# Two-block transformer on one core: products with weights' rounded parts first, and weight splits held behind a norm's scalings

## The chip, the cores and the metric

The kernel runs on one core of a Trainium2 chip. The time is the device time of one execution in microseconds (us). The engines that matter are TensorE (PE in the profile, its weight loads PEld), VectorE (DVE), ScalarE (ACT), GpSimd (POOL) and SyncE (SP), which issues the weight loads from memory.

## The reference, cut to what matters

A batch of one with 256 positions of width 1024 goes through two layers of a first block (retention and a sparse attention with three branches, then a gated feed-forward of 2816) and two layers of a second block (three attentions A, B and C, then a feed-forward of 4096 and a gated embedding). All is float32. What sets the time is the chain of projections, each of the form `norm(x) @ W` or `f @ W`:

```python
h = rms_norm(x, norm_mix_g[i])
proj = h @ w_in[i]
...
x = x + mixed.astype(x.dtype)
h = rms_norm(x, norm_ffn_g[i])
a, b = jnp.split(h @ w_ffn_in[i], 2, axis=-1)
x = x + ((jax.nn.silu(a) * b) @ w_ffn_out[i]).astype(x.dtype)
```

## The kernel before, in words

**Products.** Every float32 weight and activation is split into a rounded high part and a low part, the rest. ScalarE copies the high part out (`whi` of a weight), and VectorE subtracts it to get the low part (`wlo`): lines 172 and 186, function `split`. A product `x @ W` is then three TensorE products in the faster float32 mode: x high by w high, x low by w high (both need `whi` alone), and x high by w low (needs `wlo`). All TensorE products stand at line 219, transposes at line 253. "High products" are below those with `whi`, "low products" those with `wlo`.

**Items.** The kernel is first written down as a list of items, each one weight tile of 128x1024 numbers (512 KB) and the products that use it: `proj_T`, `proj_T2`, `proj_N`, `proj_H` and `Down` make them. `execute` walks over the list. Ahead of item i it loads and splits weights of later items: up to LOOK = 2 beyond the current one, with five buffers for loaded weights (NB_RAW), freed by the low part, and six for split ones (NB_HI), and at a norm's turn at most PAST_TURN = 3 past it. `proj_T2` makes the two feed-forwards' first products: per tile of 128x128 a high product of 512 columns (x high and x low side by side in `HL`) and a low product of 256 columns.

**Norms.** `Down.ends` finishes a projection back into x. Its second column half comes for rows t=0 first (four items with weights) and then for rows t=1 (four items that reuse them). After each, `norm().add(t, 1, ...)` adds to x on VectorE, squares on ScalarE, lets GpSimd raise to the power -1/2 (line 242) and scales x on VectorE (`scale`, line 197, two instructions that make `w`). `turn(t)` then transposes the scaled rows on TensorE and splits them into x high (ScalarE) and x low (VectorE), both in `xt`. `turn(0)` stands before the last item of t=1; `turn(1)` before the last of the four t=0 items of the next projection. That next projection is written with rows t=0 first and t=1 after (`tmajor`), and its t=1 half begins five products after the transposes of `turn(1)`.

**Order.** Attention heads and the like are generators ("beside") that are pumped after each item, by a planner that adds up costs per engine (`eng`). The framework lays each engine's instructions out in one fixed queue, by the order written and by its own estimate of what is ready; `tc.issue_after(q)` puts what it encloses behind q on q's engine. Each engine then takes its queue in that order.

Of the kernel before, what the change touches and what calls it, by code (L numbers as in the profile page):

```python
# [82 lines left out]

LOOK, PAST_TURN = 2, 3
CMP_STEP, RAW_LOOK = 3, 6
TAIL = 8
BEHIND = 3
# [13 lines left out]
def tile_kernel(ctx: ExitStack, tc: tile.TileContext, A: dict, out: bass.AP):  # L103
# [254 lines left out]
    def do(fn, *a):  # L358
        items.append(Item(lambda pc: fn(*a)))

    order_after = []
    raw_free = [0.0] * NB_RAW

    def arrival():
# [29 lines left out]
    def execute():  # L394
        n = len(items)
        raws = [i for i in range(n) if items[i].spec is not None and items[i].spec[-1]]
        specs = [i for i in range(n) if items[i].spec is not None and not items[i].spec[-1]]
        end = {i: i for i in specs}
        for i, it in enumerate(items):
            if it.held is not None:  # L400
                end[it.held] = i
        nxt, live = 0, []
        for i, it in enumerate(items):
            live = [j for j in live if end[j] >= i]
            while raws and raws[0] <= i + RAW_LOOK:
                j = raws.pop(0)
                items[j].pc = load(items[j].spec)
            while nxt < len(specs) and i >= lead:
                j = specs[nxt]
                ahead = sum(1 for q in specs[max(0, nxt - LOOK - 8):nxt] if q >= i)  # L410
                if items[j].pc is None:
                    items[j].pc = load(items[j].spec)
                if j > i and (len(live) >= NB_HI or ahead > LOOK):
                    break
                turn = next((q for q in turns if i <= q < j), None)
                if turn is not None and sum(1 for q in specs if turn < q < j) >= (FIRST if turn == lead else PAST_TURN):
                    break
                items[j].pc = split_weight(items[j].pc, items[j].spec)
                live.append(j)
                nxt += 1  # L420
            it.fn(it.pc)
            if it.spec is not None or it.held is not None:
                bg.pump()
# [37 lines left out]
    def proj_T2(w2d, c0, x, evac):  # L461


        box = {}
        for k0 in range(0, 8, 4):
            def fn(pc, k0=k0):
                if k0 == 0:
                    box["b"] = [bank([128, 2, 256]) for _ in range(2)]
                hi, lo = pc
                for k in range(4):  # L470
                    kk = k0 + k
                    for ct in range(2):
                        cs = slice(128 * ct, 128 * ct + 128)
                        o = box["b"][ct]
                        mm(o, hi[:, k, cs], S[x].HL(kk), kk == 0, False)
                        mm(o[:, 0, :], lo[:, k, cs], S[x].H(kk), False, kk == 7)
                if k0:
                    evac(box["b"])

            items.append(Item(fn, spec(w2d, 128 * k0, 4, c0, 256)))  # L480
# [8 lines left out]
    def proj_T(w2d, c0, ncols, x, nkt, evac, r0=0, runs=1, stride=0, pre=None):  # L489


        cw = 256 // runs
        for ci, c in enumerate(range(0, ncols, cw)):
            box = {}
            for k0 in range(0, nkt, 4):
                nk = min(4, nkt - k0)

                def fn(pc, ci=ci, k0=k0, nk=nk, box=box):
                    if pre is not None:
                        pre(k0)  # L500
                    if k0 == 0:
                        box["b"] = bank([128, 2, 256])
                    hi, lo = pc
                    xx = S[x]
                    for k in range(nk):
                        kk = k0 + k
                        for ct in range(2):
                            cs = slice(128 * ct, 128 * ct + 128)
                            wh, wl = hi[:, k, cs], lo[:, k, cs]
                            o = box["b"][:, ct, :]  # L510
                            mm(o, wh, xx.H(kk), kk == 0 and ct == 0, False)
                            mm(o, wh, xx.L(kk), False, False)
                            mm(o, wl, xx.H(kk), False, kk == nkt - 1)
                    if k0 + nk == nkt:
                        evac(ci, box["b"])

                items.append(Item(fn, spec(w2d, r0 + 128 * k0, nk, c0 + c, cw, runs, stride)))

    def part_N(acc, xx, kk, nkt, t, pc, k, first):
        hi, lo = pc  # L520
        s = slice(128 * t, 128 * t + 128)
        mm(acc, xx.H(kk)[:, s], hi[:, k, :], first, False)
        mm(acc, xx.H(kk)[:, s], lo[:, k, :], False, False)
        mm(acc, xx.L(kk)[:, s], hi[:, k, :], False, kk == nkt - 1)

    def proj_N(w2d, c0, c, x, nkt, evac, runs=1, stride=0, tmajor=False, between=None, turn=None, pre=None):

        n = c * runs
        npk = 1024 // n
        box = {}
        ks = [(k0, min(npk, nkt - k0)) for k0 in range(0, nkt, npk)]
        held = []

        def fn(pc, j, k0, nk, tt_):
            if tmajor and j == len(ks) - 1 and tt_ == (0,) and between is not None:
                between()
            if pre is not None:  # L540
                pre(k0)
            for t in tt_:
                if k0 == 0:
                    box[t] = bank([128, n])
                for k in range(nk):
                    part_N(box[t], S[x], k0 + k, nkt, t, pc, k, k0 + k == 0)
                if k0 + nk == nkt:
                    evac(t, box[t])

        for j, (k0, nk) in enumerate(ks):  # L550
            items.append(Item(lambda pc, a=(j, k0, nk): fn(pc, *a, (0,) if tmajor else (0, 1)),
                              spec(w2d, 128 * k0, nk, c0, c, runs, stride)))
            held.append(len(items) - 1)
        if tmajor:
            for j, (k0, nk) in enumerate(ks):
                if j == len(ks) - 1 and turn is not None:
                    turn()
                items.append(Item(lambda pc, a=(j, k0, nk), src=items[held[j]]: fn(src.pc, *a, (1,)), None, held[j]))

    def proj_H(w2d, c0, ncols, x, nkt, evac):  # L560

        for ci, c in enumerate(range(0, ncols, 256)):
            box = {}
            for k0 in range(0, nkt, 4):
                def fn(pc, ci=ci, k0=k0, box=box):
                    if k0 == 0:
                        box["b"] = bank([128, 2, 256])
                    for t in range(2):
                        for k in range(4):
                            part_N(box["b"][:, t, :], S[x], k0 + k, nkt, t, pc, k, k0 + k == 0 and t == 0)  # L570
                    if k0 + 4 == nkt:
                        evac(ci, box["b"])

                items.append(Item(fn, spec(w2d, 128 * k0, 4, c0 + c, 256)))

    class Down:

# [3 lines left out]
            self.w, self.n, self.tail = w2d, nkt, tail  # L581
            self.acc = None

        def part(self, k, f, pc, kk, t, c, cs):
            if self.acc is None:
                self.acc = [[bank([128, 512]) for _ in range(2)] for _ in range(2)]
            hi, lo = pc
            s = slice(128 * t, 128 * t + 128)
            o = self.acc[t][c]
            mm(o, f.H(k)[:, s], hi[:, kk, cs], k == 0, False)  # L590
            mm(o, f.H(k)[:, s], lo[:, kk, cs], False, False)
            mm(o, f.L(k)[:, s], hi[:, kk, cs], False, k == self.n - 1)

        def bulk(self, ks, f):

            for k in ks:
                def fn(pc, k=k):
                    for t in range(2):
                        for c in range(2):
                            self.part(k, S[f], pc, 0, t, c, slice(512 * c, 512 * c + 512))  # L600
                items.append(Item(fn, spec(self.w, 128 * k, 1, 0, 1024)))

        def ends(self, f, norm, turn=None, pre=None):
# [5 lines left out]
            for j in pairs:  # L609
                def fn(pc, j=j):  # L610
                    if pre is not None:
                        pre(j)
                    for kk in range(2):
                        for t in range(2):
                            self.part(j + kk, S[f], pc, kk, t, 0, whole)
                items.append(Item(fn, spec(self.w, 128 * j, 2, 0, 512)))
            for t in range(2):
                do(lambda t=t: norm().add(t, 0, self.acc[t][0]))
# [1 line left out]
            for t in range(2):  # L620
                for i, j in enumerate(pairs):
                    def fn(pc, j=j, t=t):
                        for kk in range(2):
                            self.part(j + kk, S[f], pc, kk, t, 1, whole)
                    if t == 0:
                        items.append(Item(fn, spec(self.w, 128 * j, 2, 512, 512)))
                        held.append(len(items) - 1)
                    else:
                        if j == pairs[-1] and turn is not None:
                            turn()  # L630
                        items.append(Item(lambda pc, fn=fn, src=items[held[i]]: fn(src.pc), None, held[i]))
                do(lambda t=t: norm().add(t, 1, self.acc[t][1]))


    x = cp.tile([128, 2, D], F32, name="x")
# [1326 lines left out]
```

## Time and profile before

| | |
|---|---|
| median of 3 runs | 2138.1 us (2137.21 to 2138.12) |
| the profiled execution's own time | 2137.64 us |
| its span, first to last instruction | 2135.7 us |
| TensorE busy | 2117.0 us (99%), 11840 products |
| VectorE busy | 1537.5 us (72%) |
| ScalarE busy | 1261.1 us (59%) |
| granted TensorE clock, mean | 0.999 |

The first line is what a change is compared by. The span is what the profile explains; 1.9 us of the profiled execution lie around it. Busy shares are means over the whole kernel.

### The profile page before, as it was taken

To read this page: it belongs to the slowest core of one execution; us is meant where nothing else is said; L and a number is where in the kernel's file an instruction comes from. 1 tells how busy PE (TensorE), PEld (TensorE's weight loads), DVE (VectorE), ACT (ScalarE), POOL (GpSimd) and SP (SyncE) were. 2 spreads that over 40 slices of the span, in tenths; PEclk is the share of its full clock that TensorE was granted. 3 is DMA by queue.
4 is the path that set the end of the run, shared out by engine and by line. 5 is a ranking of instruction groups with operands and counts; after the bars stand their busy time and mean duration, and the time that the engine had idled before them with its cause. 6 is when DMAs were issued, how large, how long until landed. Compare 5 with 4: busy or idle time off the path is not lost.

```text
span 2135.7 us, 32031 instructions
## 1 busy us (share of the span) xinstructions
PE 2117.0 (99%) x11840; PEld 1802.1 (84%) x11840; DVE 1537.5 (72%) x2912; ACT 1261.1 (59%) x2156; POOL 95.3 (4%) x113
## 2 busy tenths in 40 slices
PE   9999999999999999999999999999999999999998
PEld 7898888888888888888888888888887988888887
DVE  6687865656677787666667898876666898867665
ACT  5476764555556677545456777755445777755443
POOL 1000000000000000000000010000000010100000
PEclk9999999999999999999999999999999999999999
DMA  9655455565675554555656545556665545556663
GB/s 287 209 161 143 145 177 180 177 189 188 207 230 162 147 153 151 168 185 179 190 187 194 169 127 170 163 170 196 190 200 161 175 130 175 160 178 185 190 188 108
DMA packets 259338, 376.13 MB, mean 176 GB/s; under 512 B 16364, under 2 KB 160764, under 8 KB 259182
## 3 DMA queue, kind: packets, MB, share of 16 engines
q1 hardware_dynamic: 257516, 369.59, 56.3%
q0 software_dynamic: 1664, 4.50, 1.2%
q8 instruction: 93, 1.52, 0.3%
q14 instruction: 63, 0.52, 0.1%
q10 hardware_dynamic: 2, 0.00, 0.0%
HBM read 372.93 MB, written 1.11 MB: 175 GB/s over the span
## 4 chain that ended last, share of the span: by engine, by line
PE 87%; DVE 8%; ACT 2%; issue 1%; POOL 1%; DMA 1%; SPq 0%; POOLq 0%; DVEq 0%; ACTq 0%
PE b L219 84%; PE b L253 3%; DVE wlo L186 2%; DVE u L186 1%; DVE w L186 1%; POOL s L242 1%; ACT w L172 1%; ACT z L172 0%; ACT whi L172 0%; DVE xt L186 0%; ACT u L172 0%; DVE w L197 0%; DVE s L211 0%; DVE z L197 0%; DVE z L206 0%
## 5 line engine op out<-in xcount | busy, mean ns | idle before, releaser
L186 DVE TENSOR_TENSOR wlo<-raw,whi 128x1024 fp32r<-128x1024 f32 (+1 forms) x670 | 815.1, 1221 | 379.6 <-ACT whi L172 375.5
L172 ACT ACTIVATE whi<-raw 128x1024 fp32r<-128x1024 f32 (+1 forms) x670 | 705.5, 1056 | 505.2 <-PE b L219 306.2
L219 PE MATMUL b<-whi,xt 128*128 128x512 f32 (+2 forms) x2240 | 655.3, 368 | 0.8 <-DVE xt L186 0.6
L219 PE MATMUL b<-xt,whi 128*128 128x256 f32 (+1 forms) x2240 | 597.1, 340 | 0.0
L219 PE MATMUL b<-whi,u 128*128 128x512 f32 x1728 | 551.4, 392 | 0.0
L219 PE MATMUL b<-xt,wlo 128*128 128x256 f32 x1664 | 468.3, 281 | 0.0
L219 PEld LDWEIGHTS b<-whi,xt 128*128 128x128 f32 x2240 | 405.2, 189 | 71.4 <-issue 6.6
L219 PEld LDWEIGHTS b<-xt,whi 128*128 128x128 f32 x2240 | 383.9, 190 | 53.9 <-issue 2.1
L219 PE MATMUL b<-wlo,xt 128*128 128x512 f32 (+2 forms) x1120 | 409.5, 366 | 1.5 <-DVE wlo L186 1.5
L219 PEld LDWEIGHTS b<-whi,u 128*128 128x128 f32 x1728 | 324.5, 188 | 68.2 <-issue 0.3
L219 PE MATMUL b<-wlo,u 128*128 128x512 f32 x864 | 336.9, 390 | 0.0
L219 PEld LDWEIGHTS b<-xt,wlo 128*128 128x128 f32 x1664 | 315.8, 190 | 1.6
L219 PEld LDWEIGHTS b<-wlo,xt 128*128 128x128 f32 x1120 | 212.2, 189 | 32.1 <-DVE wlo L186 3.3
L219 PEld LDWEIGHTS b<-wlo,u 128*128 128x128 f32 x864 | 162.4, 188 | 30.9
L172 ACT ACTIVATE w<-b 128x256 f32<-128x256 f32 (+3 forms) x238 | 104.0, 442 | 132.9 <-PE b L219 132.4
L172 ACT ACTIVATE u<-b 64x512 fp32r<-64x512 f32 (+3 forms) x210 | 119.2, 578 | 41.3 <-PE b L219 17.8
L172 ACT ACTIVATE z<-z,s 128x256 f32<-128x256 f32 (+2 forms) x304 | 123.4, 424 | 23.2 <-DVE s L206 22.7
L242 POOL TENSOR_TENSOR s<-s,mhalf 128x1 f32<-128x1 f32 (+3 forms) x58 | 67.9, 1171 | 1478.9 <-DVE s L197 863.5
L186 DVE TENSOR_TENSOR w<-b,w 128x256 f32<-128x256 f32 x138 | 58.1, 421 | 31.0 <-ACT w L172 30.7
L186 DVE TENSOR_TENSOR u<-b,u 64x512 fp32r<-64x512 f32 (+2 forms) x110 | 72.4, 658 | 7.7 <-ACT u L172 5.6
L253 PE MATMUL b<-const,w 128*128 128x128 f32 (+2 forms) x480 | 72.0, 277 | 5.2 <-DVE w L197 4.2
L253 PEld LDWEIGHTS b<-const,w 128*128 128x128 f32 (+2 forms) x480 | 55.5, 140 | 22.3 <-issue 9.3
(157 smaller groups left out, 1463.6 us busy)
## 6 DMA issues: line engine op xcount, KB each, us to landing
raw<-w_in SPq DMA_DIRECT2D x268, 512.0 KB, 3.8
raw<-w_ffn_in SPq DMA_DIRECT2D x80, 512.0 KB, 3.6
raw<-w_up SPq DMA_DIRECT2D x64, 512.0 KB, 3.7
raw<-w_down SPq DMA_DIRECT2D x64, 512.0 KB, 3.6
raw<-w_ffn_out SPq DMA_DIRECT2D x44, 512.0 KB, 3.6
raw<-w_o_ret SPq DMA_DIRECT2D x32, 512.0 KB, 3.7
raw<-w_out SPq DMA_DIRECT2D x32, 512.0 KB, 3.7
raw<-w_o_nsa SPq DMA_DIRECT2D x16, 512.0 KB, 3.5
```

The costliest lines, as they stand in the source:

```text
L172: nc.scalar.activation(o, i, func, bias=bias, scale=scale, accum_out=accum_out)
L186: nc.vector.tensor_tensor(out=out, in0=in0, in1=in1, op=op)
L219: nc.tensor.matmul(o, lhsT, rhs, start=start, stop=stop, skip_group_check=True)
L242: nc.gpsimd.tensor_tensor(o, i, mhalf[:, :n], op=OP.pow)
L253: nc.tensor.transpose(o, i, C("ident")[:i.shape[0], :i.shape[0]])
```

## The change

Two things change. First, the order of products inside an item: all high products of an item now come before its low products. In `proj_T2` the eight high products of 512 columns come first, and then the eight low ones of 256. Second, the splits around norms: a new list `scales` holds the places of the additions `norm().add(t, 1, ...)`, and `execute` splits at most PAST_SCALE = 1 weight past such a place until it has passed it; after each, `hold_splits` makes later low parts stand behind VectorE's last instruction so far. `execute` looks for weights to split before it runs an item, `hold_splits` included.

```diff
+LOOK, PAST_TURN, PAST_SCALE = 2, 3, 1
...
+                scale = next((q for q in scales if i <= q < j), None)
+                if scale is not None and sum(1 for q in specs if scale < q < j) >= PAST_SCALE:
+                    break
                 items[j].pc = split_weight(items[j].pc, items[j].spec)
...
 # proj_T2
-                for k in range(4):
-                    kk = k0 + k
-                    for ct in range(2):
-                        cs = slice(128 * ct, 128 * ct + 128)
-                        o = box["b"][ct]
-                        mm(o, hi[:, k, cs], S[x].HL(kk), kk == 0, False)
-                        mm(o[:, 0, :], lo[:, k, cs], S[x].H(kk), False, kk == 7)
+                tiles = [(k, ct, slice(128 * ct, 128 * ct + 128)) for k in range(4) for ct in range(2)]
+                for k, ct, cs in tiles:
+                    mm(box["b"][ct], hi[:, k, cs], S[x].HL(k0 + k), k0 + k == 0, False)
+                for k, ct, cs in tiles:
+                    mm(box["b"][ct][:, 0, :], lo[:, k, cs], S[x].H(k0 + k), False, k0 + k == 7)
...
+    def parts_N(accs, xx, k0, nk, nkt, pc):
+
         hi, lo = pc
+        tiles = [(acc, k, slice(128 * t, 128 * t + 128), first and k == 0)
+                 for t, acc, first in accs for k in range(nk)]
+        for acc, k, s, first in tiles:
+            mm(acc, xx.H(k0 + k)[:, s], hi[:, k, :], first, False)
+        for acc, k, s, _ in tiles:
+            mm(acc, xx.L(k0 + k)[:, s], hi[:, k, :], False, False)
+        for acc, k, s, _ in tiles:
+            mm(acc, xx.H(k0 + k)[:, s], lo[:, k, :], False, k0 + k == nkt - 1)
...
+    def hold_splits():
+        order_after[:] = [last_of(mybir.EngineType.DVE)]
...
 # Down.ends, for t in range(2), after its items
+                scales.append(len(items))
                 do(lambda t=t: norm().add(t, 1, self.acc[t][1]))
+                do(hold_splits)
```

`proj_T`, `proj_N`, `proj_H` and `Down` have their products put in the same way (`part_N` and `Down.part` give way to `parts_N` and `Down.parts`). The counts of instructions on every engine stay as they were.

**VectorE at a norm.** The place is the norm between the first layer's attention and its feed-forward, from the addition to x for t=1 (`x_74<-x_74,b_4056`) to the low parts of the scaled rows t=1 (`xt_4047`, `xt_4048`). `wlo_...` are low parts of weights, in the order in which TensorE uses them, `s_...` the norm's sum, and `w_...<-x_74,s_...` the two scalings. Before:

```order
L186 TENSOR_TENSOR wlo_4212<-raw_4185,whi_4211 128x1024
L186 TENSOR_TENSOR xt_4047<-b_4230,xt_4047 128x4x128
L186 TENSOR_TENSOR xt_4048<-b_4237,xt_4048 128x4x128
L186 TENSOR_TENSOR x_74<-x_74,b_4056 128x512
L186 TENSOR_TENSOR wlo_4269<-raw_4215,whi_4268 128x1024
L197 SCALAR_TENSOR_TENSOR s_4253<-s_4052 128x1
L186 TENSOR_TENSOR wlo_4281<-raw_4272,whi_4280 128x1024
L197 SCALAR_TENSOR_TENSOR w_4257<-x_74,s_4254,u_4049 128x512
L197 SCALAR_TENSOR_TENSOR w_4259<-x_74,s_4254,u_4049 128x512
L186 TENSOR_TENSOR wlo_4293<-raw_4284,whi_4292 128x1024
L186 TENSOR_TENSOR xt_4047<-b_4298,xt_4047 128x4x128
L186 TENSOR_TENSOR xt_4048<-b_4305,xt_4048 128x4x128
```

The same place in the changed kernel:

```order
L186 TENSOR_TENSOR xt_4048<-b_4223,xt_4048 128x4x128
L186 TENSOR_TENSOR x_74<-x_74,b_4056 128x512
L186 TENSOR_TENSOR wlo_4248<-raw_4172,whi_4247 128x1024
L197 SCALAR_TENSOR_TENSOR s_4239<-s_4052 128x1
L186 TENSOR_TENSOR wlo_4255<-raw_4251,whi_4254 128x1024
L197 SCALAR_TENSOR_TENSOR w_4243<-x_74,s_4240,u_4049 128x512
L197 SCALAR_TENSOR_TENSOR w_4245<-x_74,s_4240,u_4049 128x512
L186 TENSOR_TENSOR wlo_4269<-raw_4258,whi_4268 128x1024
L186 TENSOR_TENSOR wlo_4281<-raw_4272,whi_4280 128x1024
L186 TENSOR_TENSOR wlo_4293<-raw_4284,whi_4292 128x1024
L186 TENSOR_TENSOR xt_4047<-b_4298,xt_4047 128x4x128
L186 TENSOR_TENSOR xt_4048<-b_4305,xt_4048 128x4x128
```

The next projection's second and third weights have moved from ahead of the addition to behind it. One low part still stands on either side of `s`, and between the scalings and the low parts of x there are now three low parts of weights where there was one. The same stands at seven norms: one before the feed-forward of each of the four layers, one between the first block's layers, and one before the gated embedding of each second-block layer.

**VectorE at the norm between the blocks.** This is the first block's final norm (`FinalNorm`), from the scalings for t=0 to those for t=1. Before:

```order
L197 SCALAR_TENSOR_TENSOR w_11575<-w_11509,s_11570,u_11424 128x512
L197 SCALAR_TENSOR_TENSOR w_11577<-w_11565,s_11570,u_11424 128x512
L186 TENSOR_TENSOR x_74<-x_74,b_10188 128x512
L186 TENSOR_TENSOR w_11614<-x_74,u_11428 128x512
L186 TENSOR_TENSOR xt_11422<-b_11668,xt_11422 128x4x128
L197 SCALAR_TENSOR_TENSOR s_11618<-s_11431 128x1
L186 TENSOR_TENSOR xt_11423<-b_11675,xt_11423 128x4x128
L197 SCALAR_TENSOR_TENSOR s_11618<-s_11618,s_11433 128x1
L186 TENSOR_TENSOR s_11618<-s_11618,s_11433 128x1
L197 SCALAR_TENSOR_TENSOR w_11624<-w_11516,s_11619,u_11424 128x512
```

Changed:

```order
L197 SCALAR_TENSOR_TENSOR w_11571<-w_11559,s_11564,u_11424 128x512
L186 TENSOR_TENSOR wlo_11619<-raw_11542,whi_11618 128x1024
L186 TENSOR_TENSOR x_74<-x_74,b_10188 128x512
L186 TENSOR_TENSOR wlo_11625<-raw_11622,whi_11624 128x1024
L186 TENSOR_TENSOR w_11602<-x_74,u_11428 128x512
L197 SCALAR_TENSOR_TENSOR s_11606<-s_11431 128x1
L186 TENSOR_TENSOR xt_11422<-b_11668,xt_11422 128x4x128
L197 SCALAR_TENSOR_TENSOR s_11606<-s_11606,s_11433 128x1
L186 TENSOR_TENSOR xt_11423<-b_11675,xt_11423 128x4x128
L186 TENSOR_TENSOR s_11606<-s_11606,s_11433 128x1
L186 TENSOR_TENSOR wlo_11713<-raw_11628,whi_11712 128x1024
L197 SCALAR_TENSOR_TENSOR w_11612<-w_11516,s_11607,u_11424 128x512
```

Two low parts of weights now stand ahead of the low parts of x for t=0 (`xt_11422<-b_11668`), and one more ahead of the scalings for t=1; behind those there are two instead of three.

**TensorE at the norm before the gated embedding.** From the transposes of `turn(1)` (`b_16286`) into the t=1 half (`b_16305`); `b_16342` belongs to the following projection. Before:

```order
L253 MATMUL b_16286<-const0_79,w_16234 128x128 x4
L219 MATMUL b_16242<-wlo_16250,xt_16045 128x512
L219 MATMUL b_16242<-whi_16249,xt_16045 128x512 x2
L219 MATMUL b_16242<-wlo_16250,xt_16045 128x512
L219 MATMUL b_16242<-whi_16249,xt_16045 128x512
L219 MATMUL b_16305<-whi_16146,xt_16044 128x512
L219 MATMUL b_16305<-wlo_16147,xt_16044 128x512
L219 MATMUL b_16305<-whi_16146,xt_16044 128x512 x2
```

Changed:

```order
L253 MATMUL b_16286<-const0_79,w_16222 128x128 x4
L219 MATMUL b_16242<-whi_16249,xt_16045 128x512 x3
L219 MATMUL b_16242<-wlo_16250,xt_16045 128x512 x2
L219 MATMUL b_16305<-whi_16146,xt_16044 128x512 x2
L219 MATMUL b_16342<-whi_16261,xt_16044 128x512 x4
L219 MATMUL b_16342<-wlo_16262,xt_16044 128x512 x2
L219 MATMUL b_16342<-whi_16273,xt_16044 128x512 x2
L219 MATMUL b_16305<-whi_16146,xt_16044 128x512 x2
```

The first product that reads x low for t=1 was the third of `b_16305` and still is (the first two read x high; before, the second was a low product). Ahead of it there now stand eight products of the following projection. This is so at the two norms before a gated embedding; between the first block's layers two small transposes and one 256-column product stand there, and at the other norms nothing.

## Rows read from the trace of the kernel before

**Rows 1.** The page, part 1: busy us, share of the span, instructions.

```profile
PE 2117.0 (99%) x11840; PEld 1802.1 (84%) x11840; DVE 1537.5 (72%) x2912; ACT 1261.1 (59%) x2156; POOL 95.3 (4%) x113
```

**Rows 2.** Who TensorE waited for: us in total, times, longest us.

```profile
PE b L253 <- DVE w L197: 4.2, 9, 0.7
PE b L219 <- DVE u L186: 2.7, 4, 1.4
...
PE b L219 <- DVE wlo L186: 1.5, 2, 0.9
```

**Rows 3.** Groups by shape: high products of `proj_T2`; low parts of weights on VectorE.

```profile
L219 PE MATMUL b<-xt,whi 128*128 128x512 f32 x1088 | 386.1, 398 | 0.0
...
L186 DVE TENSOR_TENSOR wlo<-raw,whi 128x1024 fp32r<-128x1024 f32 x664 | 809.0, 1222 | 379.1 <-ACT whi L172 375.1 <-DMA raw<-w_in 1.5 <-issue 0.3
```

**Rows 4.** Timeline of TensorE in `proj_T2` (start, us, what): nine pairs between these rows.

```profile
412.71 0.40 PE L219 MATMUL b<-xt,whi 128*128 128x512 f32 x1
412.94 0.28 PE L219 MATMUL b<-xt,wlo 128*128 128x256 f32 x1
...
415.89 0.40 PE L219 MATMUL b<-xt,whi 128*128 128x512 f32 x1
```

**Rows 5.** Timeline of TensorE, 512 columns throughout: 12 products from first to last start.

```profile
2108.07 0.62 PE L219 MATMUL b<-whi,xt 128*128 128x512 f32 x2
...
2110.79 0.39 PE L219 MATMUL b<-whi,xt 128*128 128x512 f32 x1
```

**Rows 6.** Timeline of TensorE, 256 columns throughout: 48 products from first to last start.

```profile
28.18 0.40 PE L219 MATMUL b<-xt,whi 128*128 128x256 f32 x2
...
33.94 0.28 PE L219 MATMUL b<-xt,whi 128*128 128x256 f32 x1
```

**Rows 7.** Timeline of VectorE at the first layer's feed-forward norm, rows t=1.

```profile
398.75 1.22 DVE L186 TENSOR_TENSOR wlo<-raw,whi 128x1024 fp32r<-128x1024 f32 x1
400.41 1.41 DVE L197 SCALAR_TENSOR_TENSOR w<-x,s,u 128x512 f32<-128x512 f32 x2 [0.44 <-POOL s L242]
401.74 1.22 DVE L186 TENSOR_TENSOR wlo<-raw,whi 128x1024 fp32r<-128x1024 f32 x1
402.88 1.28 DVE L186 TENSOR_TENSOR xt<-b,xt 128x512 fp32r<-128x512 f32 x2
```

**Rows 8.** Timeline of TensorE at the same norm.

```profile
401.31 0.63 PE L253 MATMUL b<-const,w 128*128 128x128 f32 x4 [0.40 <-DVE w L197]
...
403.38 0.63 PE L219 MATMUL b<-whi,xt 128*128 128x512 f32 x2
...
404.07 0.62 PE L219 MATMUL b<-whi,xt 128*128 128x512 f32 x2
```

**Rows 9.** Timeline at the norm between the blocks.

```profile
1154.62 0.68 DVE L186 TENSOR_TENSOR xt<-b,xt 128x512 fp32r<-128x512 f32 x1
...
1155.36 0.72 PE L219 MATMUL b<-whi,xt 128*128 128x512 f32 x2 [0.45 <-DVE xt L186]
...
1162.49 0.73 PE L219 MATMUL b<-whi,xt 128*128 128x512 f32 x2 [0.19 <-DVE xt L186]
```

**Rows 10.** Timeline at the last of the seven norms: VectorE's low parts of x, TensorE's first use.

```profile
2113.15 1.28 DVE L186 TENSOR_TENSOR xt<-b,xt 128x512 fp32r<-128x512 f32 x2
...
2114.34 0.62 PE L219 MATMUL b<-whi,xt 128*128 128x512 f32 x2
```

**Rows 11.** Timeline of TensorE after the second layer's feed-forward norm.

```profile
974.91 0.44 PE L253 MATMUL b<-const,w 128*128 128x128 f32 x2 [0.90 <-DVE w L186]
```

**Rows 12.** Timeline of GpSimd: the power for rows t=0 and t=1 of the first norm.

```profile
392.26 0.56 POOL L242 TENSOR_TENSOR s<-s,mhalf 128x1 f32<-128x1 f32 x1 [63.12 <-DVE s L197]
398.92 1.46 POOL L242 TENSOR_TENSOR s<-s,mhalf 128x1 f32<-128x1 f32 x1 [6.10 <-DVE s L197]
```

**Rows 13.** DMA issues of the page, part 6: count, KB each, median us to landing.

```profile
raw<-w_ffn_in SPq DMA_DIRECT2D x80, 512.0 KB, 3.6
```

**Rows 14.** TensorE in the second block's heads: a timeline row, then two windows (busy us, granted clock).

```profile
1855.98 2.05 PE L219 MATMUL b<-u 128*128 128x128 f32 x11 [1.40 <-DVE u L186]
...
1853.40:1856.80 3.40, 1.72 (x14) 1.37 (x13) 3.33 (x4) 3.36 (x7) 0.00 (x0) 1.00 0.45 164
1856.80:1860.20 3.40, 3.40 (x12) 2.92 (x12) 3.32 (x19) 3.19 (x11) 0.00 (x0) 0.50 0.65 207
```

More of the change, by code (lines that the diff above doesn't have):

```diff
@@ L82 @@
 NB_RAW, NB_HI, NB_U, NB_X, NB_Z, NB_W, NB_S = 5, 6, 13, 2, 6, 8, 24
-LOOK, PAST_TURN = 2, 3
+LOOK, PAST_TURN, PAST_SCALE = 2, 3, 1
 CMP_STEP, RAW_LOOK = 3, 6
@@ L359, in do @@
         items.append(Item(lambda pc: fn(*a)))
-    order_after = []
+    order_after, scales = [], []
     raw_free = [0.0] * NB_RAW
@@ L504, in fn @@
                     xx = S[x]
[L505 to L513, printed above, removed]
+                    tiles = [(k, ct, slice(128 * ct, 128 * ct + 128)) for k in range(nk) for ct in range(2)]
+                    for k, ct, cs in tiles:
+                        mm(box["b"][:, ct, :], hi[:, k, cs], xx.H(k0 + k), k0 + k == 0 and ct == 0, False)
+                        mm(box["b"][:, ct, :], hi[:, k, cs], xx.L(k0 + k), False, False)
+                    for k, ct, cs in tiles:
+                        mm(box["b"][:, ct, :], lo[:, k, cs], xx.H(k0 + k), False, k0 + k == nkt - 1)
                     if k0 + nk == nkt:
@@ L517, in proj_T @@
                 items.append(Item(fn, spec(w2d, r0 + 128 * k0, nk, c0 + c, cw, runs, stride)))
-    def part_N(acc, xx, kk, nkt, t, pc, k, first):
+    def parts_N(accs, xx, k0, nk, nkt, pc):
         hi, lo = pc
[L521 to L524, printed above, removed]
+        tiles = [(acc, k, slice(128 * t, 128 * t + 128), first and k == 0)
[6 more added lines that the diff above has]
+            mm(acc, xx.H(k0 + k)[:, s], lo[:, k, :], False, k0 + k == nkt - 1)
     def proj_N(w2d, c0, c, x, nkt, evac, runs=1, stride=0, tmajor=False, between=None, turn=None, pre=None):
@@ L544, in fn @@
                     box[t] = bank([128, n])
[L545 to L548, printed above, removed]
+            if k0 + nk < nkt:
+                parts_N([(t, box[t], k0 == 0) for t in tt_], S[x], k0, nk, nkt, pc)
+                return
+            for t in tt_:
+                parts_N([(t, box[t], k0 == 0)], S[x], k0, nk, nkt, pc)
+                evac(t, box[t])
         for j, (k0, nk) in enumerate(ks):
@@ L567, in fn @@
                         box["b"] = bank([128, 2, 256])
-                    for t in range(2):
-                        for k in range(4):
-                            part_N(box["b"][:, t, :], S[x], k0 + k, nkt, t, pc, k, k0 + k == 0 and t == 0)
+                    parts_N([(t, box["b"][:, t, :], k0 == 0 and t == 0) for t in range(2)], S[x], k0, 4, nkt, pc)
                     if k0 + 4 == nkt:
@@ L582, in __init__, with parts @@
             self.acc = None
-        def part(self, k, f, pc, kk, t, c, cs):
+        def parts(self, f, pc, parts):
             if self.acc is None:
@@ L587, in part @@
             hi, lo = pc
[L588 to L592, printed above, removed]
+            parts = [(self.acc[t][c], k, kk, slice(128 * t, 128 * t + 128), cs) for k, kk, t, c, cs in parts]
+            for o, k, kk, s, cs in parts:
+                mm(o, f.H(k)[:, s], hi[:, kk, cs], k == 0, False)
+                mm(o, f.L(k)[:, s], hi[:, kk, cs], False, False)
+            for o, k, kk, s, cs in parts:
+                mm(o, f.H(k)[:, s], lo[:, kk, cs], False, k == self.n - 1)
         def bulk(self, ks, f):
@@ L597, in fn @@
                 def fn(pc, k=k):
-                    for t in range(2):
-                        for c in range(2):
-                            self.part(k, S[f], pc, 0, t, c, slice(512 * c, 512 * c + 512))
+                    self.parts(S[f], pc, [(k, 0, t, c, slice(512 * c, 512 * c + 512))
+                                          for t in range(2) for c in range(2)])
                 items.append(Item(fn, spec(self.w, 128 * k, 1, 0, 1024)))
@@ L612, in fn @@
                         pre(j)
-                    for kk in range(2):
-                        for t in range(2):
-                            self.part(j + kk, S[f], pc, kk, t, 0, whole)
+                    self.parts(S[f], pc, [(j + kk, kk, t, 0, whole) for kk in range(2) for t in range(2)])
                 items.append(Item(fn, spec(self.w, 128 * j, 2, 0, 512)))
@@ L622, in fn @@
                     def fn(pc, j=j, t=t):
-                        for kk in range(2):
-                            self.part(j + kk, S[f], pc, kk, t, 1, whole)
+                        self.parts(S[f], pc, [(j + kk, kk, t, 1, whole) for kk in range(2)])
                     if t == 0:
```

## Prediction, made before the changed kernel ran

> **What bounds the kernel now.** I read the page's busy times first: TensorE works for 2117.0 of 2135.7 us [rows 1], so the time is TensorE's time plus its gaps. The reader should see there that nothing saved on another engine counts unless TensorE waits for it. The table of its waits says who it waits for: VectorE's scaled rows ahead of the transposes (4.2 us, 9 times), heads' tiles (2.7 us), and low parts of weights (1.5 us, 2 times) [rows 2]. The counts of instructions stay, so the change can act in three ways: the pitch of TensorE's products, a wait removed, a wait made. The timelines at the norms then show how near to a wait TensorE already is there.
>
> **Pitch in the feed-forwards' first products.** There are 1088 high products of 512 columns in `proj_T2` [rows 3], each followed by a low one of 256. Nine such pairs take 415.89 − 412.71 = 3.18 us, 0.353 us a pair [rows 4]. Where 512 follows 512, twelve products take 2110.79 − 2108.07 = 2.72 us, 0.2267 each [rows 5]; where 256 follows 256, 48 take 33.94 − 28.18 = 5.76 us, 0.120 each [rows 6]. Unmixed, a pair would be 0.347, about 6 ns less. Now eight of one kind are followed by eight of the other, so one of eight pairs keeps its edge: 1088 × 7/8 = 952 pairs × 5.8 ns = **−5.5 us**. The bounds are 0 (another place may give another pitch) and −6 (all pairs).
>
> The Trainium skill (TensorE: Matmul & The Clock Gate, section "Wait — 56ns, not 53.3ns?") gives a product's pitch at the full clock as its columns over 2.4 GHz plus some 2.5 ns, whatever stands beside it. By that rule the pair's price doesn't depend on order and this term would be 0; the rows show 13 ns over the columns for both kinds, not 2.5, so here the trace decides, but the rule has its rival below.
>
> **Low parts needed later inside an item.** The first low product now stands behind the item's high products, so a low part that was late has more time. The two waits of 1.5 us together, 0.9 the longest [rows 2], fall within the eight high products that now stand ahead (1.8 us): **−1.5 us**, bounds 0 and −3 (some of the heads' waits as well).
>
> **The low parts of x at a norm.** Here the order speaks against the change. In the row of the first feed-forward norm, VectorE scales the rows t=1 (`w`, from 400.41), makes one weight's low part (401.74) and then x low (402.88) [rows 7]. In the changed order three weights' low parts stand between the scalings and x low. Each takes 1.22 us [rows 3], so x low comes 2 × 1.22 = 2.44 us later. That the name of the change says "behind the scalings" helps little: the scalings themselves have one low part behind `x` and one behind `s`, as before, so they are no earlier.
>
> TensorE can stand little of it. Its third and fourth product of the t=1 half start at 404.07 [rows 8], and the first of these reads x low. The first of the two x low instructions ends half-way, at about 402.88 + 0.68 = 403.56 (0.68 is one such instruction's time [rows 9]), so there are 404.07 − 403.56 = 0.51 us of slack. The last of the seven norms shows the same: 2113.15 + 0.68 = 2113.83 against 2114.34, 0.51 [rows 10]. The new wait is 2.44 − 0.51 = 1.93, with the refilling of TensorE about **2.0 us**. By norm:
> - first-layer feed-forward norm, and the two of the second block: nothing new stands ahead; 2.0 each, 6.0.
> - between the first block's layers: two small transposes and a 256-column product ahead hide 0.3; 1.7.
> - second layer's feed-forward norm: TensorE waits 0.90 us a little later for a scaled tile [rows 11]; with the refilling some 1.1 of the 2.0 is time it would have waited anyway; 0.9.
> - the two before a gated embedding: eight products of the next projection (8 × 0.2267 = 1.8 us) stand ahead now; about 0.25 each, 0.5.
> - between the blocks: x low for t=0 begins at 1154.62 and TensorE waited 0.45 us for it [rows 9]. Two low parts (2.4 us) now stand ahead of it, so this wait grows to some 2.9. For t=1 it waited 0.19 at 1162.49 [rows 9]; its scalings have one more low part ahead and two instead of three behind, so that end of the chain is about 2.2 later; 2.2 in all.
>
> Sum: **+11.3 us**. Bounds are 0 (if TensorE doesn't stand still there) and 15 (2.2 at every place, no cover).
>
> **The wait ahead of the transposes stays.** TensorE waits 0.40 us for `w` at 401.31 [rows 8]. GpSimd's power takes 0.56 us for t=0, with VectorE idle, and 1.46 for t=1, beside a weight's low part [rows 12]. Since one low part still stands right behind `s`, I change nothing: 0. The Trainium skill (SBUF — State Buffer, section "Who interferes with whom") says that a VectorE instruction with two inputs in SBUF and a GpSimd one that reads SBUF block each other for the whole instruction. The trace agrees: the low part ran from 398.75 to about 399.97, and the power beside it came out at 1.46 instead of 0.56.
>
> **Loads.** A tile's load waits for a buffer that a low part frees, and takes 3.6 us [rows 13]. The latest low parts at the norm end at about 402.96, 404.2 and 405.4 (1.22 apart from the third on), so loads behind them land at 406.6, 407.8 and 409.0. The tiles are split behind x low, which now ends at 406.6, in steps of 1.22 with two earlier tiles ahead: 0, each us of lateness costing one, 7 us at worst over seven norms.
>
> **Clock and heads.** TensorE's granted clock fell once: after waits of 1.40 us and a shorter one, at 1855.98, the next 3.4 us ran at 0.50 [rows 14], that is 1.7 us lost. A single wait of 0.90 [rows 11] brought no fall. Six new waits are of about 2 us or longer, beyond the 1.40 that had one. I count two falls, **+3.4 us**; bounds 0 and 10.2. The planner moves heads by one to six items; their present waits (2.7 us [rows 2]) and the 1.7 of the clock may go or come again: 0, bounds −6 and +6.
>
> **Sum.** 2137.64 (the profiled execution) − 5.5 − 1.5 + 11.3 + 3.4 = 2145.3; the median of the runs shown is 0.46 above the profiled one, so 2145.8.
>
> **The rivals.** What a measurement can tell from no change is about 0.2%, 4.3 us: below 2133.8 is faster, above 2142.4 slower.
> - *Clock falls at every long wait.* For it: all six are longer than the 1.40 ahead of the one fall. Against: that one followed two waits close together, in a stretch where TensorE worked less than half [rows 14]. 6 × 1.7 instead of 3.4: 2145.8 + 6.8 = 2152.6.
> - *No saving of pitch.* The three pitches [rows 4 to 6] come from three places, so the 6 ns may belong to place and not to order. Then 2145.8 + 5.5 = 2151.3. This is also the time by the skill's rule on pitch.
> - *The power gets short.* If the low part behind `s` starts late (its high part is later on ScalarE), the power meets an idle VectorE and takes 0.56 instead of 1.46. All behind it on VectorE comes 0.9 us earlier: 0.9 at each of five norms bound by x low and 0.56 (0.40 and the refilling) at the two others, 5.6 us: 2140.2, no change to be told. Against: the order still has it there.
> - *x low is not waited for, and it is faster.* If the two low parts moved ahead of x low fit into time in which VectorE would stand idle, nothing is lost at norms, nor by the clock: 2137.64 − 5.5 − 1.5 + 0.46 = 2131.1. It decides at a delay of x low under 0.51 us instead of 2.44. For it: 0.4 us of idle time on VectorE ahead of `w`. Against: behind `w` VectorE runs without a gap [rows 7].
>
> **How the numbers follow.** The main case (two-us waits, some falls of the clock, saved pitch) has 0.52; its own range is 2140 to 2150, of which I give 0.42 above 2142.4 and 0.10 below. The clock at every wait 0.15, no pitch 0.08, short power 0.15, faster 0.10. Slower is 0.42 + 0.15 + 0.08 = 0.65, the same 0.10 + 0.15 = 0.25, faster 0.10. The range leaves out the faster case and the worst of clock, loads and heads together (some 0.08): from 2136, 4 under the short power for the heads, to 2157, 4 above the clock's case. The number is the main case's.
>
> **What would show it.** In the changed kernel's trace TensorE should wait for `xt` on VectorE six or so times for about 2 us, where the 0.45 and 0.19 stand now; three rows of `wlo` should stand between `w` and `xt` on VectorE; `proj_T2` should show runs of eight at 0.227 and eight at 0.120 us; waits for `wlo` should be gone; the power for t=1 should still take 1.46; and stretches behind the long waits should show whether the clock fell to 0.50. I am wrong if x low comes no later than now, if pitch doesn't fall, or if falls of the clock, lateness of loads or heads outweigh the norms.

## The result, and the profile after

The changed kernel takes 2156.8 us (2154.0 to 2158.5, 4 runs) against 2137.8 of before: ratio 1.009, 95% interval 1.0077 to 1.0103. It is slower, as forecast, but by 19 us where 8 were forecast, and its median lies at the upper end of the range of 2136 to 2157.

TensorE's own work hardly grew (page, part 1, beside [rows 1]):

```profile
PE 2118.2 (98%) x11840; PEld 1807.6 (84%) x11840; DVE 1535.1 (71%) x2912; ACT 1265.1 (59%) x2156; POOL 93.8 (4%) x113
```

Who TensorE waited for after the change (us in total, times, longest us), beside [rows 2]:

```profile
PE b L219 <- DVE u L186: 10.5, 7, 2.6
PE b L219 <- DVE xt L186: 9.8, 6, 2.4
PE b L253 <- DVE w L197: 4.4, 9, 0.9
PE b L219 <- ACT z L172: 2.4, 1, 2.4
```

The waits for low parts of weights are gone, and six waits for x low have come. The waits for the heads' tiles `u` have grown from 2.7 to 10.5 us, and one of 2.4 for `z` is new; the sum had this growth at nothing.

**The norm.** VectorE, GpSimd and TensorE of the changed kernel at the first feed-forward norm (timeline: start, us, what, idle ahead and its releaser), beside [rows 7, 8, 12]:

```profile
400.93 1.42 DVE L197 SCALAR_TENSOR_TENSOR w<-x,s,u 128x512 f32<-128x512 f32 x2 [0.44 <-POOL s L242]
402.26 3.49 DVE L186 TENSOR_TENSOR wlo<-raw,whi 128x1024 fp32r<-128x1024 f32 x3
405.67 1.28 DVE L186 TENSOR_TENSOR xt<-b,xt 128x512 fp32r<-128x512 f32 x2
```

```profile
399.42 1.48 POOL L242 TENSOR_TENSOR s<-s,mhalf 128x1 f32<-128x1 f32 x1 [6.09 <-DVE s L197]
```

```profile
401.83 0.63 PE L253 MATMUL b<-const,w 128*128 128x128 f32 x4 [0.36 <-DVE w L197]
...
404.13 0.61 PE L219 MATMUL b<-whi,xt 128*128 128x512 f32 x2
406.40 0.72 PE L219 MATMUL b<-whi,xt 128*128 128x512 f32 x2 [1.66 <-DVE xt L186]
```

Three low parts stand between `w` and `xt`, and TensorE waits 1.66 us idle, that is 2.27 from product pair to product pair where two products after one another take 0.45. The wait ahead of the transposes is still there (0.36 for 0.40), and so is the long power (1.48 for 1.46).

**The pitch** (the time from one product's start to the next one's). TensorE in `proj_T2`, beside [rows 4]:

```profile
414.68 2.10 PE L219 MATMUL b<-xt,whi 128*128 128x512 f32 x8
416.62 1.11 PE L219 MATMUL b<-xt,wlo 128*128 128x256 f32 x8
417.56 2.00 PE L219 MATMUL b<-xt,whi 128*128 128x512 f32 x8
419.41 1.11 PE L219 MATMUL b<-xt,wlo 128*128 128x256 f32 x8
```

Eight pairs take 419.41 − 416.62 = 2.79 us, 0.349 a pair against 0.353.

**Where the 17.7 us of span went.** Both programs run the same 9856 products with weights, so the difference of the start times of the k-th of them shows where time is lost. Read at the ends of stretches:

| stretch (time in the kernel before) | change in us |
|---|---|
| the norms: 395 to 409, 579 to 592, 967 to 976, 1145 to 1170, 1428 to 1447, 1605 to 1634, 1920 to 1944, 2086 to 2121 | +1.9, +1.7, +0.9, +2.7, +1.8, +0.2, +2.3, +0.1: **+11.6** |
| feed-forwards: 409 to 579, 976 to 1145, 1447 to 1605, 1944 to 2086 | −1.6, −1.5, −1.1, −1.5: **−5.7** |
| attention of the first block, two layers | +0.5, +0.6: **+1.1** |
| attention of the second block: 1170 to 1428, 1634 to 1920 | +6.3, +4.5: **+10.8** |

The first two rows stand beside the forecast's +11.3 and −5.5. The first holds more than waits, though: at the norm between the blocks the products fall behind from 4.1 to 5.7 us while the clock is low (the first window below), so some 1.6 of its +2.7, and of the 11.6, belong to the clock. Without them the norms cost 10.0. The last row the forecast did not have.

**The clock.** Windows of TensorE in the changed kernel (us, then busy us of PE, PEld, DVE, ACT and POOL with counts, the granted clock, DMA share, GB/s), beside [rows 14]:

```profile
1160.30:1163.70 3.40, 3.40 (x10) 2.62 (x9) 2.81 (x5) 2.00 (x4) 1.55 (x1) 0.50 0.64 177
1225.20:1228.60 3.40, 3.40 (x14) 2.41 (x11) 2.16 (x3) 1.43 (x2) 0.00 (x0) 0.50 0.99 296
1358.30:1361.70 3.40, 3.40 (x10) 2.72 (x10) 3.40 (x19) 3.20 (x15) 0.00 (x0) 0.50 0.00 0
1788.40:1795.20 6.80, 5.12 (x14) 4.16 (x15) 6.65 (x16) 4.12 (x7) 0.00 (x0) 0.50 0.26 78
406.40:409.80 3.40, 3.40 (x16) 2.79 (x17) 2.42 (x4) 2.34 (x3) 0.00 (x0) 1.00 0.93 328
```

17 us ran at half of 2.4 GHz, which costs 8.5, against 3.4 us and 1.7 before. Only the first window follows a norm's wait (the longest, 2.35, right behind another of 0.25); after the wait at 406.40, as after the other four at norms, the clock stayed at 1.00. The others lie in the heads: 6.8 us lost there against 1.7 before, which is 5.1 of the second block's 10.8.

### The profile page after: what moved, and what is told of

Same layout as the page of the kernel before. It is cut to its first block, busy times and chain, and to the rows that moved or that the text cites. A ratio compares the mean times of both kernels' runs of the same rounds, so it can differ in the third digit from the quotient of the medians.

```text
span 2153.4 us, 32145 instructions
## 1 busy us (share of the span) xinstructions
PE 2118.2 (98%) x11840; PEld 1807.6 (84%) x11840; DVE 1535.1 (71%) x2912; ACT 1265.1 (59%) x2156; POOL 93.8 (4%) x113
## 3 DMA queue, kind: packets, MB, share of 16 engines
q8 instruction: 93, 1.52, 0.3%
## 5 line engine op out<-in xcount | busy, mean ns | idle before, releaser
L186 DVE TENSOR_TENSOR wlo<-raw,whi 128x1024 fp32r<-128x1024 f32 (+1 forms) x670 | 814.4, 1221 | 407.3 <-ACT whi L172 400.5
L219 PE MATMUL b<-whi,xt 128*128 128x512 f32 (+2 forms) x2240 | 525.2, 371 | 10.0 <-DVE xt L186 9.8
L219 PEld LDWEIGHTS b<-whi,xt 128*128 128x128 f32 x2240 | 381.3, 191 | 78.5 <-DVE xt L186 12.9
L219 PE MATMUL b<-whi,u 128*128 128x512 f32 x1728 | 442.7, 393 | 0.0
L219 PE MATMUL b<-xt,whi 128*128 128x256 f32 (+1 forms) x2240 | 423.5, 336 | 0.0
L219 PEld LDWEIGHTS b<-xt,whi 128*128 128x128 f32 x2240 | 341.8, 190 | 41.2 <-ACT whi L172 2.5
L219 PEld LDWEIGHTS b<-whi,u 128*128 128x128 f32 x1728 | 317.7, 188 | 63.8 <-issue 2.1
L219 PE MATMUL b<-wlo,xt 128*128 128x512 f32 (+2 forms) x1120 | 281.2, 365 | 0.0
L219 PE MATMUL b<-wlo,u 128*128 128x512 f32 x864 | 240.3, 389 | 0.0
L219 PE MATMUL b<-xt,wlo 128*128 128x256 f32 x1664 | 232.5, 282 | 0.0
L219 PEld LDWEIGHTS b<-xt,wlo 128*128 128x128 f32 x1664 | 222.7, 191 | 10.6
L219 PEld LDWEIGHTS b<-wlo,xt 128*128 128x128 f32 x1120 | 195.1, 190 | 34.9 <-DVE xt L186 0.6
L219 PEld LDWEIGHTS b<-wlo,u 128*128 128x128 f32 x864 | 162.2, 188 | 34.0
L186 DVE TENSOR_TENSOR u<-b,u 64x512 fp32r<-64x512 f32 (+2 forms) x110 | 72.2, 658 | 18.1 <-ACT u L172 16.8
L172 ACT ACTIVATE w<-x 128x512 f32<-128x512 f32 x40 | 25.1, 628 | 58.2 <-DVE x L186 54.6
```

Source lines behind the costliest of these rows:

```text
L172: nc.scalar.activation(o, i, func, bias=bias, scale=scale, accum_out=accum_out)
L186: nc.vector.tensor_tensor(out=out, in0=in0, in1=in1, op=op)
L219: nc.tensor.matmul(o, lhsT, rhs, start=start, stop=stop, skip_group_check=True)
```

## The experiments

Times are medians beside runs of the kernel before on the same chip (2137.4 to 2137.5). "Steps of before" means that the planner's calls run down a recorded list, and no longer decide:

```diff
         def pump(self):
             self.fill()
-            p0 = eng["P"]
-            while eng["P"] - p0 < PUMP_PE and max(eng["V"], eng["A"]) < eng["P"] + BACKLOG:
...
+            for z in STEPS[self.calls].split():
...
+                    self.advance(next(g for g in self.first + self.active if g[2] == int(n)))
```

The list adds 30 lines, so L219 reads L249 there, and L186 L216. In the list of before and that of the changed kernel, 384 of 731 steps stand at another item, by up to ten; with the second part alone the list is that of before, so all of these moves come from the new order of products.

**First part alone.**

```diff
-                scale = next((q for q in scales if i <= q < j), None)
...
-                do(hold_splits)
+                do(lambda: None)
```

> The first part alone: products in the new order, no scales and no hold_splits (an empty item stands in its place). Theory 'heads': by the new order the planner starts heads' steps at other items, and the waits and falls of the clock this brings in the second block and the second layer cost some 12 us; the norms' late x low, some 10, is gone. So 2137.8 - 5.1 + 12 = about 2145 us (2141 to 2149), with waits for u and z of 2 us in the heads as in the changed kernel and no long wait for xt. Rival 'norms': the norms' waits are the source of the falls of the clock and of the heads' lateness as well, so without them only the pitch's gain is left: about 2132 us.

Measured 2145.3 us, ratio 1.0038 (1.0025 to 1.005). The norms are gone from the waits and the heads are not:

```profile
PE b L219 <- DVE u L186: 10.8, 7, 2.6
PE b L253 <- DVE w L197: 4.4, 9, 0.9
PE b L219 <- ACT z L172: 2.4, 1, 2.4
```

So the norms' waits do not cause the heads' ones.

**Second part alone** (the `scales` and `hold_splits` lines of the change on the kernel before).

> The second part alone: scales and hold_splits on the products of before. The planner takes the same steps at the same items as before. Theory 'heads': the norms' 10 to 11 us, without the pitch's gain and with one or two falls of the clock more: 2149 us (2146 to 2153), six waits for xt of 1 to 2.4 us, the heads' waits as before. Rival 'norms': about 2160 us (the changed kernel's 2156.8 without the pitch's saving of some 5), with the long waits in the heads too.

Measured 2150.4 us, ratio 1.0064 (1.005 to 1.0077). The norms alone cost 12.9; with the first part's 7.9 that makes 20.8, near the whole's 19. Without the new order of products the weights' low parts, moved behind the addition, are late too:

```profile
PE b L219 <- DVE xt L186: 6.7, 6, 2.4
PE b L219 <- DVE wlo L186: 5.3, 16, 0.8
```

**The whole change with the steps of before.**

> The changed kernel in full, but the planner's decisions (which head takes a step after which item) are replaced by a list of those it took in the kernel before. Theory 'heads': 2156.8 less the heads' 12 us = 2145 us (2142 to 2149), the sum of the prediction without its miss; waits for xt stay, those for u and z are as before. Rival 'norms': within 3 us of 2156.8. A third, 'order': the products' order itself (a group of eight products in a row, with head products between groups only) delays the heads, whatever the planner decides: 2150 or more.

Measured 2152.0 us, ratio 1.0067 (1.0054 to 1.0079), in the range of the third theory. Only some 5 us come back.

**First part with the steps of before.**

> The first part alone, with the planner's decisions of the kernel before. Theory 'heads': only the pitch's saving is left: 2137.8 - 5.1 = 2132.7 us (2131 to 2136), faster than both kernels. 'order': the same as the first part alone, 2141 to 2149. 'norms' gives 2132 as well.

Measured 2139.0 us, ratio 1.0007 (0.9998 to 1.0016): no gain, though the feed-forwards show theirs. A miss by 6 us for 'heads', and below the range of 'order' too: the order of products costs beside heads even where the planner's steps stand still, and the moved steps cost 6.3 more (2145.3 less 2139.0). Its 1.6 and the second part's 12.9 make 14.5, which is what the whole change with the steps of before costs (14.6). One place where the order costs, TensorE at a head of the second block's first layer (the kernel before waits 0.67 there, at 1366.27):

```profile
1364.70 0.33 PE L249 MATMUL b<-u 128*128 128x128 f32 x1 [0.60 <-ACT u L202]
1366.42 1.79 PE L249 MATMUL b<-u 128*128 128x128 f32 x11 [1.40 <-DVE u L216]
```

**The planner's steps of the changed kernel alone**, on the order of products of before.

> The kernel before, order of products and splits as before, but the planner's steps replaced by the list of those it took in the changed kernel. If the moved steps themselves cost what tells the first part alone (2145.3) from the first part with the steps of before (2139.0), this is 2137.4 + 6.3 = 2143.7 us (2142 to 2146), with waits of 2 us and more for z and u in the second block. Rival, that the steps cost only together with the new order of products (they were planned for it): 2137 to 2140.

Measured 2146.4 us, ratio 1.0044 (1.0031 to 1.0056), just above the range. The moved steps cost 8.9 us by themselves. What they do is seen at one head; TensorE:

```profile
1213.37 1.10 PE L249 MATMUL b<-u,later 128*128 128x512 f32 x6
1214.94 0.49 PE L249 MATMUL b<-u,later 128*128 128x512 f32 x1 [0.47 <-ACT u L202]
1216.37 0.97 PE L249 MATMUL b<-u,later 128*128 128x512 f32 x5 [0.94 <-DVE u L216]
...
1222.44 2.31 PE L249 MATMUL b<-z,V 128*64 128x256 f32 x16 [2.13 <-ACT z L202]
```

and ScalarE in the same run:

```profile
1219.31 1.28 ACT L202 ACT_TABLE_LOAD   x1
1220.60 1.06 ACT L202 ACTIVATE u<-u 128x1024 f32<-128x1024 f32 x1
1221.56 1.56 ACT L202 ACTIVATE z<-z 128x768 f32<-128x768 f32 x2
```

Two steps of six products run together, and so do the two of eight that read their result `z`. Between them stand 2.7 us of weights' products, while ScalarE, which comes to them only at 1219.31, needs a table load and three activations, 3.9 us. In the kernel before, the steps alternated and the same tiles were not waited for:

```profile
1211.19 1.17 PE L219 MATMUL b<-u,later 128*128 128x512 f32 x6
...
1216.10 1.11 PE L219 MATMUL b<-u,later 128*128 128x512 f32 x6
...
1219.87 0.88 PE L219 MATMUL b<-z,V 128*64 128x256 f32 x8
...
1225.04 0.88 PE L219 MATMUL b<-z,V 128*64 128x256 f32 x8
```

**The new order in one kind of item.** First `proj_T2` alone.

> The kernel before with the new order of products in proj_T2 alone. No heads run beside those items, and the planner takes its steps at the same items as before. If the pitch falls by the term of the prediction, 2137.5 - 5.5 = 2132 us (2131 to 2133.5), faster. Rival, that the order doesn't matter to the pitch: 2137.5.

Measured 2134.0 us, ratio 0.9984 (0.9975 to 0.9993): faster, by 3.4, and half a microsecond short of the range. By the table's method the four feed-forwards gain 5.8, and heads give some back: 0.7 near 1300, 0.9 at 1366 and, net, 1.0 between 1660 and 1800, all where the engines' instructions stand in the order of before. What differs ahead of the second of these places: GpSimd's power and VectorE's low part beside it, 37 us earlier in the kernel before:

```profile
1329.19 1.64 POOL L242 TENSOR_TENSOR s<-s,mhalf 128x8 f32<-128x8 f32 x1 [5.53 <-DVE s L191]
1329.34 1.23 DVE L186 TENSOR_TENSOR wlo<-raw,whi 128x1024 fp32r<-128x1024 f32 x1 [0.29 <-issue]
```

and in this one:

```profile
1326.59 1.23 DVE L186 TENSOR_TENSOR wlo<-raw,whi 128x1024 fp32r<-128x1024 f32 x1
1326.80 2.51 POOL L242 TENSOR_TENSOR s<-s,mhalf 128x8 f32<-128x8 f32 x1 [5.53 <-DVE s L191]
```

Where the power starts first it takes 1.64 us, where the low part does, 2.51. VectorE's next step needs it: up to here VectorE ran 2.75 us ahead of the kernel before, from here 1.52, and so it does until TensorE waits for it at 1366. The other two places were not taken apart. Then `proj_T` alone, and `proj_N` with `proj_H`, both with the steps of before.

> The kernel before with the new order of products in proj_T alone, the planner's steps as before. The first part with the planner's steps of before took 2139.0 us, that of proj_T2 alone 2134.0: some 5 us must come from the other items. Theory: any group of high products lets TensorE reach a head's step earlier than VectorE and ScalarE have it, so both kinds of items beside heads lose: here 1 to 3 us, 2138.5 to 2140.5. Rival, that proj_T doesn't matter: 2136.5 to 2138.

> The same for proj_N and proj_H alone. Theory: 2 to 4 us lost, 2139.5 to 2141.5, with a wait of 1.4 us or more for u near 1366, where the profile of the first part with the planner's steps of before has it. Rival, that they don't matter: 2136.5 to 2138.

`proj_T` 2139.2 us, ratio 1.0007 (0.9998 to 1.0016), too near to its rival to tell; `proj_N` and `proj_H` 2142.8 us, ratio 1.0024 (1.0015 to 1.0034), with the 0.60 and 1.40 of idle time at 1369 that the first part with the steps of before has at 1366. This is above the range, and in the profiles of both runs the clock fell to 0.50 for 3.4 us behind the wait of 1.40 (at 1369.75 and 1367.53), 1.7 us more. So the second is where the order itself costs.

**The norm's three places for low parts.** First `hold_splits` without `scales`, the old order of products.

> The kernel before with hold_splits alone, no scales and the old order of products. At the norms no low part stands between the addition for t=1 and its scalings, three between the scalings and x low. If the power is long because of the low part beside it (theory 'power'), it takes 0.56 us instead of 1.46, the scalings and transposes come about 1 us and 0.56 us earlier, and the wait for x low is 1.3 to 1.5 us instead of the 1.8 to 1.9 of the changed kernel: 0.9 more than before at five norms, nothing or less at the two before a gated embedding, 2141 to 2144 us. Rival, that the power is long for another reason: transposes still wait 0.4, x low comes 2.4 us late: 2148 or more, as with the second part alone.

Measured 2143.7 us, ratio 1.003 (1.0019 to 1.0042). GpSimd's power for t=1 at the first norm, beside [rows 12]:

```profile
399.13 0.55 POOL L242 TENSOR_TENSOR s<-s,mhalf 128x1 f32<-128x1 f32 x1 [6.34 <-DVE s L197]
```

With no low part beside it the power is short: the theory 'power' holds. The Trainium skill's rule on the two engines' shared port, which the prediction cites (SBUF — State Buffer, "Who interferes with whom"), is borne out for the power that starts second; the last section has a case where the subtraction starts second and isn't held up. Then one low part behind the scalings and two behind x low (`hold_splits` after the addition for t=1 only):

```diff
+                if left:
+                    if j > i and left[0] == 0:
+                        break
+                    left[0] -= 1
                 items[j].pc = split_weight(items[j].pc, items[j].spec)
...
     def second_turn():
         S["turn"].turn(1)
+        if left:
+            left.clear()
+            order_after[:] = [last_of(mybir.EngineType.DVE)]
...
+    def hold_splits():
+        order_after[:] = [last_of(mybir.EngineType.DVE)]
+        left[:] = [1]
```

> The kernel before with the old order of products; after the addition for t=1 one weight is split behind the scalings, the other two behind the low parts of x for t=1. By 'power' nothing is late any more: the transposes' wait of 0.40 (0.56 with the refilling) is gone at seven norms and x low has its slack: 2137.5 - 3.9 = 2133.6 us (2132.5 to 2135). Rival: within 1 us of 2137.5.

Measured 2137.1 us, ratio 1.0 (0.9991 to 1.0008): a miss. The transposes start at 400.79 without a wait, and right behind them TensorE waits for the low part that now is late:

```profile
400.79 1.08 PE L253 MATMUL b<-const,w 128*128 128x128 f32 x8
401.63 0.47 PE L219 MATMUL b<-whi,xt 128*128 128x512 f32 x1
402.35 0.50 PE L219 MATMUL b<-wlo,xt 128*128 128x512 f32 x1 [0.25 <-DVE wlo L186]
402.69 0.64 PE L219 MATMUL b<-whi,xt 128*128 128x512 f32 x2
403.17 0.40 PE L219 MATMUL b<-wlo,xt 128*128 128x512 f32 x1
403.40 0.62 PE L219 MATMUL b<-whi,xt 128*128 128x512 f32 x2
```

The t=1 half starts at 403.40, where it started before (403.38 [rows 8]). With `proj_T2`'s order added:

> The last with the new order in proj_T2 too. If the two gains are apart from each other, 2137.5 - 5.5 - 3.9 = 2128 us (2127 to 2130), faster than both kernels; if the slack won at norms is used up by the pitch, between that and 2132.

Measured 2133.2 us, ratio 0.998 (0.9971 to 0.9989), outside both ranges and hardly more than `proj_T2` alone gains. So the low products of the norm's items have to come later, too; the last version does that, with the steps of before:

```diff
+                if tmajor:
+                    parts_N([(t, box[t], k0 == 0)], S[x], k0, nk, nkt, pc)
+                else:
```

> The version with the power alone and the new order in proj_T2 (2133.2 us), with the new order also in those items of proj_N that stand at a norm, and the planner's steps of before. In the version with the power alone, the half microsecond won ahead of the transposes was waited again for one weight's low part, at 402.35 and the same place of the other norms; with its low products last this wait should go: 2133.2 - 7 x 0.5 = 2129.7 us (2128.5 to 2132). Rival, that the won time is lost elsewhere at the norm: 2133.

Measured 2129.9 us, ratio 0.9965 (0.9952 to 0.9977), as expected, and faster than both kernels. By the table's method the norms gain 3.7 us here, where the version before it gained 0.7. At the first norm TensorE runs through:

```profile
402.13 1.10 PE L283 MATMUL b<-const,w 128*128 128x128 f32 x8
402.99 1.18 PE L249 MATMUL b<-whi,xt 128*128 128x512 f32 x4
404.01 0.62 PE L249 MATMUL b<-wlo,xt 128*128 128x512 f32 x2
```

## Why the prediction went right and wrong

- **Low parts of x at a norm: right in mechanism and places, and near in size.** +10.0 us of the span, without the fall of the clock, for +11.3; six waits, 2.35 us at the norm between the blocks (2.9 forecast), almost nothing at the two before a gated embedding. The second part alone shows the same by time.
- **Pitch: right in mechanism.** −5.7 for −5.5. The rival that order doesn't matter falls with 0.349 against 0.353 us and with `proj_T2` alone; the Trainium skill's rule on pitch (TensorE: Matmul & The Clock Gate, section "Wait — 56ns, not 53.3ns?") does not hold here. That the size came out so well is in part luck: the prediction's own rows give 0.3533 − 0.3467, 6.7 ns a pair and not 5.8, that is −6.3 us, and −7.3 for all pairs.
- **Low parts later in an item: right**, the waits are gone. Both (0.65 at 1766.46 and 0.89 at 1777.37 in the kernel before) stood among the second block's heads, so the −1.5 can't be told apart from what the heads lost.
- **The wait ahead of the transposes: right**, and the cause, one low part beside the power, is now shown by taking it away.
- **The step that failed: "Clock and heads", where "The planner moves heads by one to six items" was put at 0 with bounds of −6 and +6.** Heads' stretches cost +11.9 us in both blocks. That is more than the norms' 10.0, which the prediction had named as a sign of being wrong. The steps moved by up to ten items. The bounds came from waits in the kernel before, and those say nothing of steps at other places. The moved steps alone cost 8.9. The order of products beside heads costs too: `proj_N` and `proj_H` 5.3. The two do not add up: with the 3.4 that `proj_T2` gains they make 10.8, and the first part, which has them all, costs 7.9.
- **The same step had two falls of the clock, +3.4, at norms.** One came there, some 1.6 us. The clock's whole loss grew by 6.8, and 5.1 of it sits in the heads, within their 11.9. That every long wait lowers the clock is wrong: one of six at norms did. The argument against it misread its row by a little: TensorE worked 1.72 of 3.40 us ahead of the fall [rows 14], just over half.

What stays open is how the order of `proj_N` and `proj_H` makes heads late with the planner's steps unchanged; it was located, not taken apart. The effects of single parts also shift by which of the power and the low part starts first, as shown above, so sums of them should hold to 2 us or so only; that figure is an estimate from the 2.6 us that heads gave back with `proj_T2` alone.

## What to carry to other kernels

Where a planner's costs decide the places of side work, a change of order that looks free changes its decisions: record its decisions before and after, run each list on the other order, and cost the moved steps like any other edit. An operation put behind a chain is only free if the work that comes behind both has slack enough; here there were 0.51 us for 2.44. A wait removed in one place is worth something only if the next wait behind it is removed as well, as the last two versions show.

## What the runs showed of the hardware

The same two instructions, a power of 8 columns on GpSimd and a subtraction of two SBUF tiles on VectorE, took 1.64 or 2.51 us for the power by which started first, some 0.2 us either way. The subtraction took 1.23 us in both. The shorter time is also that of such a power with VectorE idle beside it, here in the kernel before:

```profile
1809.97 1.64 POOL L242 TENSOR_TENSOR s<-s,mhalf 128x8 f32<-128x8 f32 x1 [42.07 <-DVE s L191]
```

So in these rows the power that starts second is held up and the subtraction that starts second is not. With the order of instructions unchanged, that took 1.2 us of VectorE's lead, and TensorE lost 0.9 by it 37 us later.
